# Staggering the K pairs of a down projection and releasing their loads product by product

## The chip, the cores and the metric

One core of a Trainium2 chip runs the whole program; seven cores are idle. The metric is the device time of one execution in microseconds. The engines are TensorE (PE in the profile, its weight loads PEld), VectorE (DVE), ScalarE (ACT), GpSimd (POOL, used here only to issue DMAs) and SyncE (SP, which issues DMAs too).

## The reference

A decoder trunk on x of 1024 tokens by 1024 channels, float32: one short-convolution layer and one attention layer (multi-head latent attention with 8 heads), each followed by a gated feed-forward block, and a final normalisation. What the change touches is the second half of the feed-forward block, which runs twice:

```python
def swiglu_ffn(h, w13, w2):
    g, u = jnp.split(h @ w13, 2, axis=-1)
    return (jax.nn.silu(g) * u) @ w2          # (1024 x 2816) @ (2816 x 1024)

h = h + swiglu_ffn(rms_norm(h, conv_ffn_norm_g[i]), conv_ffn_w13[i], conv_ffn_w2[i])
h = h + swiglu_ffn(rms_norm(h, mla_ffn_norm_g[j]), mla_ffn_w13[j], mla_ffn_w2[j])
```

## The kernel before

Activations are kept transposed: 128 channels on the partitions, 1024 tokens along the row, in tiles of 4 KB a partition. Every float32 operand is split into a high and a low float32r part, so one product of two blocks is three matmuls (high·high, high·low, low·high).

Feed-forward products go by a seven-product scheme (Strassen's, in Winograd's form) on 2 by 2 blocks: a **K pair** (256 of the inner dimension), two output blocks of 128 channels and two token halves of 512. `pair()` (line 145) does one **step**: for two output blocks it runs through the seven products in the order of `SEQ` (1, 5, 6, 2, 7, 3, 4), and in each through the K pairs that it is given. A step over three K pairs is 7 x 3 x 3 = 63 matmuls of 128x512, over two pairs 42. For each product `source()` mixes the four raw weight blocks on VectorE (tiles `w` and `sums`; line 155 adds two of them, 158, 161 and 165 subtract), `split()` casts the result on ScalarE (line 92) and takes the rest on VectorE (line 93) into `wo`, and after the matmuls `hook()` takes the bank away. Products 1, 6, 7 and 4 follow each other in the bank of tile `ps_z` and 5 and 3 in that of `ps_y`: the next product adds to the same bank, so TensorE can't start it before `hook()` has read the bank. Weight blocks are loaded by SP (line 140) into `wraw`, 10 tiles of 2 KB, of which a step with three pairs takes 5.

`ffn()` (line 682) first makes the inner activations: `up()` runs once for each of 22 blocks of 128 inner channels (a step over four K pairs, 84 matmuls), and after each second block `operands()` (line 256) puts eleven small VectorE instructions, with casts on ScalarE, on `queue`; `drip()` takes one from there after each product. They make the seven operands `x` of one K pair, which POOL stores to memory (`md`, 512 KB each). The last pair made (`KEPT`, pair 4) stays on chip.

`back()` (line 475) is the down projection, 11 K pairs by 8 output blocks, 16 steps. `GROUPS` cuts the pairs into (0,1), (2,3,4), (5,6,7), (8,9,10); each group runs through four steps (`mp`, two output blocks each) before the next group starts. In the first group ScalarE copies four of the seven products into `h` and VectorE adds three; later VectorE adds all seven (line 500). While a group runs, the operands of the next are asked for (`xm` from `md`, on POOL's queue, line 85): some after each step, the rest after the fourth. All these tiles share 41 slots (`NSLOT`): a load whose slot isn't free waits on POOL's queue for the matmul that reads it last. In the third group SP also loads `hs`, the residual.

The order on each engine is made at compile time by a scheduler that simulates the engines' times; a tile's next load waits for its last reader by a semaphore. POOL and SP issue in order; all transfers share 16 DMA engines.

Of the kernel before, what the change touches and what calls it, by code (L numbers as in the profile page):

```python
# [36 lines left out]
GROUPS = ((0, 1), (2, 3, 4), (5, 6, 7), (8, 9, 10))  # L37
KEPT = 4
PREFETCH = 4
# [15 lines left out]
def trunk(ctx, tc, aps, out):  # L55
# [28 lines left out]
    def move(dst, src):  # L84
        nc.gpsimd.dma_start(dst, src)  # L85
# [44 lines left out]
    def raw_blocks(w, kps, c1, c2):  # L130

        nk = len(kps)
        wv = w.rearrange("(k h p) n -> p h k n", p=P, h=2)
        R = {}
        for q, (kh, c, key) in enumerate(((0, c1, "11"), (0, c2, "12"), (1, c2, "22"), (1, c1, "21"))):
            if nk > 2 or q % 2 == 0:
                t = wraw("w" + key)
            else:
                t = t[:, HS // 2:]
            nc.sync.dma_start(t[:, :nk * P].rearrange("p (k m) -> p k m", m=P), wv[:, kh, kps[0]:kps[0] + nk, c:c + P])  # L140
            R[key] = t
        return R

    def pair(w, kps, X, c1, c2, hook, seq=SEQ):
# [27 lines left out]
        for name in seq:  # L172
            o = wop("wo" + name)
            hi, lo = part(o, n)
            split(hi, lo, source(name))
# [8 lines left out]
            hook(name, b)  # L184
            drip(1 if len(queue) < 14 else 2)

    def blocks(w, X, c1, c2, emit, seq=SEQ):
# [3 lines left out]
        def hook(name, b):  # L191
            if name in "156":
                kept[name] = half("z" + name)
                nc.scalar.copy(out=kept[name], in_=b)  # L194
            elif name == "2":
                emit("11", b, kept["1"])
            elif name == "3":
                emit("12", b, kept["6"])
            elif name == "7":
                emit("22", b, kept["5"])  # L200
            else:
                emit("21", b, None)
# [27 lines left out]
    def take(dst, ps, add):  # L230
        if add is None:
            nc.scalar.copy(out=dst, in_=ps)
        else:
            nc.vector.tensor_tensor(dst, ps, add, ALU.add)  # L234
# [240 lines left out]
    def back(w, load, st, final, ready, kept):  # L475
# [3 lines left out]
        for gi, g in enumerate(GROUPS):  # L479
            todo = []  # L480
            if gi + 1 < len(GROUPS):
                nxt = GROUPS[gi + 1]
                new = [{} for _ in nxt]
                if KEPT in nxt:
                    new[nxt.index(KEPT)] = kept
                todo = [(i, kp, name) for name in SEQ for i, kp in enumerate(nxt) if kp != KEPT]
            pace = -(-(NSLOT - KD - 2 - 7 * (len(g) + (gi == 0))) // 3)
            for mp in range(KD // 2):
                n1, n2 = 2 * mp, 2 * mp + 1
                if gi == 0:  # L490
                    st[n1], st[n2] = slot("h"), slot("h")
                h1, h2 = st[n1], st[n2]
                dst = {"1": h1[:, T1], "2": h1[:, T1], "6": h1[:, T2], "3": h1[:, T2],
                       "7": h2[:, T2], "5": h2[:, T2], "4": h2[:, T1]}

                def hook(name, b):
                    if gi == 0 and name in "1654":
                        nc.scalar.copy(out=dst[name], in_=b)
                    else:
                        nc.vector.tensor_tensor(dst[name], b, dst[name], ALU.add)  # L500
                    if gi == len(GROUPS) - 1 and name == "3":
                        final(mp, 2)

                pair(w2, g, ready, n1 * P, n2 * P, hook)
                n = len(todo) if mp == KD // 2 - 1 else min(len(todo), pace)
                for i, kp, name in todo[:n]:
                    new[i][name] = load(kp, name)
                todo = todo[n:]
                if gi == len(GROUPS) - 2:
                    for m in (n1, n2):  # L510
                        t = slot("hs")
                        nc.sync.dma_start(t, hd[m])
                        queue.append(lambda m=m, t=t: nc.vector.tensor_tensor(st[m], st[m], t, ALU.add))
                if gi == len(GROUPS) - 1:
                    final(mp, 1)
            if gi + 1 < len(GROUPS):
                ready = new
                drip()

# [162 lines left out]
    def ffn(w13, w2, X, after, side=None):  # L682
# [3 lines left out]
        def load(kp, name):  # L686
            o = slot("xm", F32R, [P, 2, HS])
            move(o, md[kp, SEQ.index(name)])
            return o

        def up(j):
# [3 lines left out]
            def emit(blk, ps, add):  # L695
                if blk in ("11", "12"):
                    take(a[:, T1 if blk == "11" else T2], ps, add)
                elif blk == "22":
                    take(u2, ps, add)
                else:  # L700
                    got["u1"] = ps
# [16 lines left out]
        ready, kept = [{} for _ in GROUPS[0]], {}  # L718
        order = [k for kp in range(KF // 2) if kp != KEPT for k in (2 * kp, 2 * kp + 1)] + [2 * KEPT, 2 * KEPT + 1]
        for j in order:  # L720
            up(j)
            if j % 2:
                put = kept.__setitem__ if j // 2 == KEPT else lambda name, o, j=j: move(md[j // 2, SEQ.index(name)], o)
# [11 lines left out]
        back(w2, load, st, after(st), ready, kept)  # L735
# [483 lines left out]
```

## Time and profile before

| | |
|---|---|
| median of 3 runs | 2104.06 us (2101.93 to 2107.01) |
| profiled execution | 2109.98 us, span of its instructions 2108.0 us |
| granted TensorE clock over the span | 0.992 |
| TensorE busy | 2071.3 us (98%) |
| VectorE, ScalarE busy | 1624.9 us (77%), 932.0 us (44%) |
| first down projection | about 779 to 989 us of the span |
| second down projection | about 1862 to 2088 us |

Times in the rows are microseconds from the start of the span, mean durations in ns. "Busy" counts an engine's instructions; a busy TensorE isn't TensorE at its peak. A granted clock of 1.00 is 2.4 GHz, half of it 1.2 GHz. A DMA share is the mean busy share of the core's 16 DMA engines, and may pass 1 where packets overlap.

### The profile page before, as it was taken

Reading aid. Unit: us, or ns where it says so; the run is one execution under the profiler, and the core shown is the slowest. Engines: PE = TensorE matmul, PEld = TensorE weight load, DVE = VectorE, ACT = ScalarE, POOL = GpSimd, SP = SyncE. Lnnn points to the kernel's source line nnn. Section 1 sums busy time; section 2 is a strip of 40 time slices with the busy share of each in tenths; the row PEclk is TensorE's granted clock in tenths of the full one; section 3 lists DMA queues with packets and bytes.
Section 4 is the critical chain, followed back from the end, with each engine's and each line's share of the span. In section 5 each row is a group of like instructions: output and inputs, shape, how many; then the busy total and the mean of one; then the engine's idle time right before and its main releaser. Section 6 shows DMA issues by size and latency. Waiting matters only on the chain.

```text
span 2108.0 us, 27158 instructions
## 1 busy us (share of the span) xinstructions
PE 2071.3 (98%) x9606; PEld 1721.6 (82%) x9606; DVE 1624.9 (77%) x2662; ACT 932.0 (44%) x1697; POOL 230.5 (11%) x440
## 2 busy tenths in 40 slices
PE   8999999999999999999999999999999999999998
PEld 6878887888888887788888888887888888878786
DVE  5797757789988887689558877767888888876775
ACT  6633344444444443224445555455444444442235
POOL 1000100000101121110001011100010010121100
PEclk9999999999999999999999999999999999999998
DMA  6133462343544587764222124532454454686751
GB/s 248 35 97 119 141 214 91 120 147 123 185 140 156 174 302 262 258 226 133 85 69 66 38 66 122 178 101 62 140 170 148 133 173 144 216 280 203 268 185 80
DMA packets 263399, 321.24 MB, mean 152 GB/s; under 512 B 18959, under 2 KB 207568, under 8 KB 263264
## 3 DMA queue, kind: packets, MB, share of 16 engines
q0 software_dynamic: 57792, 201.46, 28.0%
q1 hardware_dynamic: 205472, 118.07, 19.0%
q8 instruction: 75, 1.23, 0.2%
q14 instruction: 60, 0.49, 0.1%
HBM read 206.22 MB, written 108.00 MB: 149 GB/s over the span
## 4 chain that ended last, share of the span: by engine, by line
PE 92%; DVE 3%; DMA 2%; ACT 1%; issue 1%; SPq 0%; POOL 0%; POOLq 0%; DVEq 0%; ACTq 0%
PE ps_z L180 37%; PE ps_y L180 27%; PE ps_c L225 7%; PE ps_s L948 4%; PE ps_pv L983 2%; PE ps_t L972 1%; PE ps_wo L105 1%; PE ps_wo L107 1%; PE ps_wo L109 1%; PE ps_l L109 1%; PE ps_l L105 1%; PE ps_l L107 1%; DMA w<-in_mla_ffn_w_dram 1%; PE ps_q L105 1%; PE ps_q L107 1%
## 5 line engine op out<-in xcount | busy, mean ns | idle before, releaser
L180 PE MATMUL ps_z<-x,wo 128*128 128x512 f32 x2532 | 609.9, 390 | 3.6 <-ACT z L194 2.8
L180 PEld LDWEIGHTS ps_z<-x,wo 128*128 128x128 f32 x2532 | 475.5, 188 | 104.7 <-ACT z L194 4.1
L180 PE MATMUL ps_y<-x,wo 128*128 128x512 f32 x1764 | 432.3, 389 | 1.2 <-DVE x L93 0.9
L180 PEld LDWEIGHTS ps_y<-x,wo 128*128 128x128 f32 x1764 | 330.6, 188 | 70.9 <-DVE x L93 1.8
L92 ACT CAST wo<-w 128x512 fp32r<-128x512 f32 (+2 forms) x423 | 238.6, 570 | 281.1 <-PE ps_y L180 110.5
L93 DVE TENSOR_TENSOR wo<-w,wo 128x512 fp32r<-128x512 f32 (+2 forms) x423 | 260.8, 623 | 62.2 <-ACT wo L92 61.4
L180 PE MATMUL ps_z<-xm,wo 128*128 128x512 f32 x960 | 241.9, 395 | 7.9 <-DVE h L500 5.9
L180 PEld LDWEIGHTS ps_z<-xm,wo 128*128 128x128 f32 x960 | 180.8, 190 | 50.5 <-DVE h L500 7.8
L92 ACT CAST wo<-sums 128x512 fp32r<-128x512 f32 (+2 forms) x172 | 98.3, 572 | 260.9 <-PE ps_y L180 101.7
L180 PE MATMUL ps_y<-xm,wo 128*128 128x512 f32 x720 | 182.6, 392 | 2.3 <-DVE h L500 2.3
L180 PEld LDWEIGHTS ps_y<-xm,wo 128*128 128x128 f32 x720 | 135.2, 189 | 31.8 <-DVE h L500 3.1
L85 POOL DMA_DIRECT2D md<-x x140 | 75.0, 536 | 738.1 <-DVE x L93 695.6
L194 ACT COPY z<-ps_z 128x512 f32<-128x512 f32 x106 | 62.0, 585 | 136.5 <-PE ps_z L180 136.4
L93 DVE TENSOR_TENSOR wo<-sums,wo 128x512 fp32r<-128x512 f32 (+2 forms) x172 | 107.4, 624 | 14.2 <-ACT wo L92 12.9
L500 DVE TENSOR_TENSOR h<-ps_z,h 128x512 f32<-128x512 f32 x104 | 71.5, 688 | 40.5 <-PE ps_z L180 39.6
L85 POOL DMA_DIRECT2D xm<-md x140 | 74.1, 536 | 260.1 <-PE ps_z L180 138.3
L93 DVE TENSOR_TENSOR x<-t,x 128x512 fp32r<-128x512 f32 x136 | 92.2, 686 | 5.7 <-ACT x L92 5.7
L234 DVE TENSOR_TENSOR a<-ps_y,z 128x512 f32<-128x512 f32 x88 | 60.7, 689 | 42.3 <-PE ps_y L180 42.1
L92 ACT CAST x<-t 128x512 fp32r<-128x512 f32 x136 | 82.4, 620 | 20.8 <-DVE t L249 20.2
L955 ACT ACTIVATE p<-ps_s,mx,qscale 128x128 f32<-128x128 f32 (+3 forms) x64 | 53.4, 835 | 70.7 <-DVE mx L954 66.7
L155 DVE TENSOR_TENSOR sums<-w,w 128x512 f32<-128x512 f32 (+2 forms) x85 | 53.3, 627 | 31.3 <-DMA w<-in_mla_ffn_w_dram 15.1
L500 DVE TENSOR_TENSOR h<-ps_y,h 128x512 f32<-128x512 f32 x88 | 60.4, 686 | 20.7 <-PE ps_y L180 20.5
(295 smaller groups left out, 3213.6 us busy)
## 6 DMA issues: line engine op xcount, KB each, us to landing
md<-x POOLq DMA_DIRECT2D x140, 512.0 KB, 3.5
xm<-md POOLq DMA_DIRECT2D x140, 512.0 KB, 8.1
w<-in_conv_ffn_w_dram SPq DMA_DIRECT2D x88, 256.0 KB, 2.9
w<-in_mla_ffn_w_dram SPq DMA_DIRECT2D x88, 256.0 KB, 3.0
w<-in_conv_w_in_dram SPq DMA_DIRECT2D x48, 256.0 KB, 3.1
hd<-h POOLq DMA_DIRECT2D x24, 512.0 KB, 3.5
w<-in_conv_ffn_w_dram SPq DMA_DIRECT2D x48, 192.0 KB, 4.7
w<-in_mla_ffn_w_dram SPq DMA_DIRECT2D x48, 192.0 KB, 4.4
```

Of the source, the lines that this page charges most:

```text
L85: nc.gpsimd.dma_start(dst, src)
L92: nc.scalar.copy(out=hi, in_=src)
L93: (eng or nc.vector).tensor_tensor(lo, src, hi.bitcast(F32), ALU.subtract)
L105: nc.tensor.matmul(ps[:, hs], lhsT=wh, rhs=xh(k)[:, hs], start=st, stop=False)
L107: nc.tensor.matmul(ps[:, hs], lhsT=wh, rhs=xl(k)[:, hs], start=False, stop=False)
L180: mm = lambda w_, x_, f: nc.tensor.matmul(b, lhsT=w_[:, m], rhs=x_, start=f, stop=True, skip_group_check=True)
L194: nc.scalar.copy(out=kept[name], in_=b)
L225: nc.tensor.matmul(ps[:, ts], lhsT=w_[:, m], rhs=X[i][f"b{kh}{th}"][:, q, :], start=st and j == 0, stop=en and j == 2)
L234: nc.vector.tensor_tensor(dst, ps, add, ALU.add)
L500: nc.vector.tensor_tensor(dst[name], b, dst[name], ALU.add)
L948: nc.tensor.matmul(ps[:, a:b], lhsT=q[:, qs], rhs=k[:, a:b], start=i == 0, stop=i == 4 and b < kw)
L955: nc.scalar.activation(p, ps[:, :kw], AF.Exp, bias=mx, scale=qscale[:, qb:qb + 1], accum_out=rsum)
```

## The change

`GROUPS` becomes `SETS`, eight sets of K pairs that run through two steps each. A pair still has four steps, one for each two output blocks, but pairs enter and leave in turn: pair 1 runs steps 2 to 5, pair 2 steps 4 to 7, and so on. Pair 10 runs in the first two steps and in the last two, so its seven operands are loaded twice. The kept pair is pair 3 in place of 4; the inner activations of pair 10 are made first, those of pair 3 last. Since `SEQ0` goes with block 0, the first `up()` now runs in the order of `SEQ`.

Loads: the operands of the first set are asked for one at a time by the products of the last two `up()` steps; the other 63 by `pace()`, load *i* after product 1.5 *i* of the down projection (*i* below 14) or 10 + 4/3 *i*. Each such load waits by a semaphore for the instruction that took that product's bank away. Before, nothing but slots held them.

In the first four steps each weight mix and split is put behind the bank reads of four products earlier on its engine (an edge for the scheduler, no semaphore), and `drip()` is called after three products of step 0 and four of each of steps 1 to 3, in place of all seven.

```diff
-GROUPS = ((0, 1), (2, 3, 4), (5, 6, 7), (8, 9, 10))
-KEPT = 4
-PREFETCH = 4
+SETS = ((0, 10), (0, 1), (1, 2, 3), (2, 3, 4), (4, 5, 6), (5, 6, 7), (7, 8, 9), (8, 9, 10))
+KEPT = 3
+AHEAD = 4
+PACE = (1.5, 10, 4 / 3)
...
+    marks, paced = [], deque()
+    @contextmanager
+    def behind(n):
+        with ExitStack() as stack:
+            seen = set()
+            for inst in reversed(marks[:max(0, len(marks) - n + 1)][-4:]):
+                if inst is not None and inst.ins.engine not in seen:
+                    seen.add(inst.ins.engine)
+                    stack.enter_context(tc.issue_after(inst.ins))
+            yield
...
-    def pair(w, kps, X, c1, c2, hook, seq=SEQ):
+    def pair(w, kps, X, c1, c2, hook, seq=SEQ, thin=SEQ, ahead=99):
...
-            split(hi, lo, source(name))
+            with behind(ahead):
+                split(hi, lo, source(name))
...
-            hook(name, b)
-            drip(1 if len(queue) < 14 else 2)
+            marks.append(hook(name, b))
+            if paced and marks[-1] is not None:
+                paced.popleft()(marks[-1])
+            if name in thin:
+                drip(1 if len(queue) < 14 else 2)
...
+        todo = []
+        for q in range(1, len(SETS)):
+            new = [k for k in SETS[q] if k != KEPT and k not in SETS[q - 1]]
+            todo += [(kp, name) for name in SEQ for kp in new]
+        nload, products = len(todo), [0]
+        def pace(i):
+            return PACE[0] * i if i < 14 else PACE[1] + PACE[2] * i
+        for t in range(2 * len(SETS)):
+            mp, kps = t % (KD // 2), SETS[t // 2]
+            first, last = t < KD // 2, t >= 2 * len(SETS) - KD // 2
...
+            def hook(name, b):
+                if first and name in "1654":
+                    done = nc.scalar.copy(out=dst[name], in_=b)
+                else:
+                    done = nc.vector.tensor_tensor(dst[name], b, dst[name], ALU.add)
...
+                while todo and pace(nload - len(todo)) <= products[0]:
+                    kp, nm = todo.pop(0)
+                    ready.setdefault(kp, {})[nm] = load(kp, nm, done)
+                products[0] += 1
+                return done
+            if t % 4 == 0 and t:
+                drip()
+            pair(w2, kps, [ready[kp] for kp in kps], n1 * P, n2 * P, hook, thin=("1", "5", "6") if t == 0 else SEQ[::2] if first else SEQ, ahead=AHEAD if first else 99)
...
-        def load(kp, name):
+        def load(kp, name, behind=None):
             o = slot("xm", F32R, [P, 2, HS])
-            move(o, md[kp, SEQ.index(name)])
+            d = move(o, md[kp, SEQ.index(name)])
+            if behind is not None:
+                tc.add_manual_dep(d.ins, behind.ins.name, SYNC)
             return o
...
-            if j == order[-3]:
+            if j in order[-3:-1]:
+                kp = SETS[0][j == order[-2]]
                 for name in SEQ:
-                    ready[0][name] = load(GROUPS[0][0], name)
-        for name in SEQ:
-            for i, kp in enumerate(GROUPS[0]):
-                if i:
-                    ready[i][name] = load(kp, name)
+                    paced.append(lambda done, kp=kp, name=name: ready[kp].__setitem__(name, load(kp, name, done)))
+        while paced:
+            paced.popleft()(None)
```

## Rows read from the trace of the kernel before

**Rows 1.** The page's first part: busy time of each engine, share, instructions.
```profile
PE 2071.3 (98%) x9606; PEld 1721.6 (82%) x9606; DVE 1624.9 (77%) x2662; ACT 932.0 (44%) x1697; POOL 230.5 (11%) x440
```

**Rows 2.** TensorE's waits, 770 to 1000 us: line, awaited; total us, times, longest.
```profile
PE ps_z L180 <- DVE h L500: 2.9, 1, 2.9
PE ps_z L180 <- ACT wo L92: 1.1, 1, 1.1
PE ps_z L180 <- DVE wo L93: 0.5, 1, 0.5
```

**Rows 3.** TensorE's waits, 1845 to 2070 us.
```profile
PE ps_z L180 <- DVE h L500: 3.0, 1, 3.0
PE ps_y L180 <- DVE h L500: 2.0, 1, 2.0
```

**Rows 4.** Busy time by stretch: us, then each engine (x), PEclk, DMA share, GB/s.
```profile
780.00:790.00 10.00, 9.76 (x42) 7.44 (x41) 9.29 (x18) 6.82 (x15) 3.69 (x7) 1.00 1.13 389
...
874.00:882.00 8.00, 8.00 (x29) 6.39 (x28) 5.28 (x11) 1.25 (x3) 1.58 (x3) 0.79 1.11 406
882.00:890.00 8.00, 8.00 (x37) 6.60 (x36) 4.83 (x9) 2.28 (x5) 1.06 (x2) 1.00 1.11 390
...
930.00:940.00 10.00, 10.00 (x46) 8.29 (x45) 7.65 (x15) 2.47 (x5) 1.45 (x3) 1.00 1.12 391
...
1870.00:1880.00 10.00, 9.24 (x32) 7.02 (x32) 8.73 (x19) 4.52 (x11) 1.05 (x2) 0.83 1.13 399
...
1959.00:1967.00 8.00, 8.00 (x30) 6.40 (x29) 5.31 (x11) 1.30 (x3) 1.60 (x4) 0.79 1.11 403
```

**Rows 5.** The chain that ended last, in order of time: start us, us, what.
```profile
863.88 8.48 DMA w<-in_conv_ffn_w_dram
...
889.45 4.08 PE ps_z L180 x18
...
1861.50 7.87 DMA w<-in_mla_ffn_w_dram
...
1948.74 8.58 DMA w<-in_mla_ffn_w_dram
```

**Rows 6.** VectorE in order of time, from 852 us; idle time and releaser bracketed.
```profile
872.48 0.56 DVE L155 TENSOR_TENSOR sums<-w,w 128x384 f32<-128x384 f32 x1 [4.39 <-DMA w<-in_conv_ffn_w_dram]
872.96 0.68 DVE L500 TENSOR_TENSOR h<-ps_z,h 128x512 f32<-128x512 f32 x1
```

**Rows 7.** POOL in order of time, 855 to 885 us.
```profile
859.11 1.19 POOL L85 DMA_DIRECT2D xm<-md  x2 [34.24 <-PE ps_z L180]
...
870.66 0.53 POOL L85 DMA_DIRECT2D xm<-md  x1 [0.15 <-issue]
```

**Rows 8.** DMA queues, 860 to 872 us: packets, MB, share of 16 engines.
```profile
q0 software_dynamic: 928, 3.41, 86.1%
q1 hardware_dynamic: 878, 0.43, 14.2%
```

**Rows 9.** Weight loads of line 140, 843 to 858 us.
```profile
DMA to landing us min/median/max: 2.6/2.6/2.6
```

**Rows 10.** All instructions on tile xm: loads from issue to landing.
```profile
DMA to landing us min/median/max: 3.4/8.1/13.2
```

**Rows 11.** Busy time by stretch: the two down projections.
```profile
779.00:989.00 210.00, 205.13 (x890) 167.48 (x889) 163.98 (x290) 73.55 (x144) 30.73 (x59) 0.99 0.70 234
1862.00:2088.00 226.00, 220.72 (x980) 179.88 (x978) 163.52 (x290) 84.68 (x165) 26.93 (x51) 0.98 0.59 196
```

**Rows 12.** VectorE by form, 779.5 to 798.5 us: count, busy us, mean ns, idle before.
```profile
L93 DVE TENSOR_TENSOR x<-t,x 128x512 fp32r<-128x512 f32 x4 | 2.7, 686 | 0.0
...
L93 DVE TENSOR_TENSOR x<-a,x 128x512 fp32r<-128x512 f32 x3 | 2.1, 686 | 0.0
```

**Rows 13.** TensorE at the first step of the first `up()`, in order of time.
```profile
359.82 3.01 PE L180 MATMUL ps_z<-x,wo 128*128 128x512 f32 x12 [1.19 <-ACT z L194]
```

More of the change, by code (lines that the diff above doesn't have):

```diff
@@ L1 @@
 from collections import deque
-from contextlib import ExitStack
+from contextlib import ExitStack, contextmanager
 import numpy as np
@@ L193, in hook @@
                 kept[name] = half("z" + name)
[L194 to L202, printed above, removed]
+                return nc.scalar.copy(out=kept[name], in_=b)
+            if name == "2":
+                return emit("11", b, kept["1"])
+            if name == "3":
+                return emit("12", b, kept["6"])
+            if name == "7":
+                return emit("22", b, kept["5"])
+            return emit("21", b, None)
         pair(w, range(len(X)), X, c1, c2, hook, seq)
@@ L472, in tables, with back @@
         move(trig[0], cos)
-    def back(w, load, st, final, ready, kept):
+    def back(w, load, st, final, ready):
         w2 = w.rearrange("a k n -> (a k) n")
[L479 to L517, printed above, removed]
-                drip()
@@ new lines, in back @@
+        todo = []
[7 more added lines that the diff above has]
+            mp, kps = t % (KD // 2), SETS[t // 2]
+            n1, n2 = 2 * mp, 2 * mp + 1
+            first, last = t < KD // 2, t >= 2 * len(SETS) - KD // 2
+            if first:
+                st[n1], st[n2] = slot("h"), slot("h")
+            h1, h2 = st[n1], st[n2]
+            dst = {"1": h1[:, T1], "2": h1[:, T1], "6": h1[:, T2], "3": h1[:, T2],
+                   "7": h2[:, T2], "5": h2[:, T2], "4": h2[:, T1]}
+            def hook(name, b):
[3 more added lines that the diff above has]
+                    done = nc.vector.tensor_tensor(dst[name], b, dst[name], ALU.add)
+                if last and name == "3":
+                    final(mp, 2)
+                while todo and pace(nload - len(todo)) <= products[0]:
[4 more added lines that the diff above has]
+            if t % 4 == 0 and t:
+                drip()
+            pair(w2, kps, [ready[kp] for kp in kps], n1 * P, n2 * P, hook, thin=("1", "5", "6") if t == 0 else SEQ[::2] if first else SEQ, ahead=AHEAD if first else 99)
+            if 8 <= t < 12:
+                for m in (n1, n2):
+                    x = slot("hs")
+                    nc.sync.dma_start(x, hd[m])
+                    queue.append(lambda m=m, x=x: nc.vector.tensor_tensor(st[m], st[m], x, ALU.add))
+            if last:
+                final(mp, 1)
@@ L696, in emit @@
                 if blk in ("11", "12"):
[L697 to L701, printed above, removed]
+                    return take(a[:, T1 if blk == "11" else T2], ps, add)
+                if blk == "22":
+                    return take(u2, ps, add)
+                got["u1"] = ps
             blocks(w, X, j * P, (KF + j) * P, emit, SEQ if j else SEQ0)
@@ L716, in up @@
             mid[j] = a
-        ready, kept = [{} for _ in GROUPS[0]], {}
-        order = [k for kp in range(KF // 2) if kp != KEPT for k in (2 * kp, 2 * kp + 1)] + [2 * KEPT, 2 * KEPT + 1]
+        ready = {kp: {} for kp in SETS[0] + (KEPT,)}
+        kpo = [SETS[0][1]] + [kp for kp in range(KF // 2) if kp not in (KEPT, SETS[0][1])] + [KEPT]
+        order = [k for kp in kpo for k in (2 * kp, 2 * kp + 1)]
         for j in order:
@@ L722, in ffn @@
             if j % 2:
-                put = kept.__setitem__ if j // 2 == KEPT else lambda name, o, j=j: move(md[j // 2, SEQ.index(name)], o)
+                put = ready[KEPT].__setitem__ if j // 2 == KEPT else lambda name, o, j=j: move(md[j // 2, SEQ.index(name)], o)
                 operands(mid.pop(j - 1), mid.pop(j), put)
```

12 lines of the change are left out of this document (6 added, 6 removed).

## The prediction

> **What bounds the kernel now.** I read the page's busy times first: TensorE is busy for 2071.3 of 2108.0 us [rows 1], so only its pauses, and stretches at a lower clock, can be won. Next its waits in the two down projections: 2.9 us at one place, 1.1 and 0.5 us at others in the first, 3.0 and 2.0 us in the second [rows 2, 3]; smaller ones are 0.2 us each. Then the clock by stretch: 0.79 over 8 us right after the first long pause, 0.83 over 10 us and 0.79 over 8 us after the two of the second projection, 1.00 in the others shown [rows 4]. A lost share of the clock is lost time: 0.21 x 8 = 1.7 us, 0.17 x 10 = 1.7 us, 1.7 us. The reader checks this by counts: 29 matmuls began in the 8 us after the pause, 37 in the next 8 [rows 4], and 8 x 4.08/18 = 8 x 0.227 us [rows 5] is 1.8 us. So the change has in reach
>
> - in the last step of the second group, once in each projection: 2.9 + 1.7 and 3.0 + 1.7 = **9.3 us**;
> - in the first steps: 1.1 + 0.5 in the first projection, 2.0 + 1.7 in the second = **5.3 us**.
>
> Why the long pauses? In the chain of waits they are weight loads: 8.48 and 8.58 us in flight, 7.87 us for that of the first steps [rows 5]; in a quiet stretch the same load lands after 2.6 us [rows 9]. VectorE sat 4.39 us on the first of them with a weight mix, and the bank read that TensorE waited for (`h<-ps_z`) stood right behind it in VectorE's order [rows 6]. The load was late because POOL had begun a run of twelve operand loads, from 859.11 to 870.66 us (the first and the last are shown), as pairs 2 and 3 left their slots together [rows 7]. In these 12 us POOL's queue moved 3.41 MB in 928 packets, SP's only 0.43 MB in 878 [rows 8].
>
> **The change part by part.**
>
> *The same work.* Old and new have four steps of two pairs and twelve of three: 4 x 42 + 12 x 63 = 924 matmuls, the same splits, the same bank reads. TensorE's floor stays.
>
> *Loads by pace.* A product is 9 matmuls, 2.04 us, with three pairs, and 6, 1.36 us, with two. One load per 4/3 products is one in 2.72 us, or in the first steps one per 1.5 products, in 2.04 us. When saturated the DMA engines move about 406 GB/s [rows 4], so a load of 512 KB (0.524 MB) holds them for 1.29 us: 47% and 63% of the time, where the old burst held them altogether. Weights ask for 0.786 MB per step of 14.3 us, 55 GB/s; hence there is room, also where `hs` adds two loads of 512 KB to a step (73 GB/s; 193 + 55 + 73 = 321 of 406). How late may a weight load be? The one of 8.48 us cost TensorE 2.9, so 5.6 us would have cost nothing. Under a burst it takes 8.5, alone 2.6; at about half the load I take the middle, 5.5, or less. That is under the limit, though barely; but the limit is the tightest one: from 930 to 940 us the engines were saturated (1.12) and TensorE was busy for all 10.00 us [rows 4]. I take the two long pauses away whole: **-9.3 us** (bounds: 0, if the bursts stay, and -9.3).
>
> *The last `up()` steps and the first steps.* Here fourteen loads, until now in two runs of seven and one of twelve behind, are spread over two `up()` steps (38 us); 780 to 790 us was at a DMA share of 1.13 [rows 4], which falls, since the twelve are spread as well. The kept pair's operands are made now while three or four, not seven, queue entries fall to a step: in 19 us VectorE did seven operand splits of 0.69 us [rows 12] besides their mixes and was busy for 9.29 of 10 us [rows 4]. With the thinner queue one operand falls into step 0, four into step 1, two into step 2; they are needed in step 4, so nothing waits for them. Step 1 stays nearly full on VectorE, so I don't take all: half of 1.6 us in the first projection, and 2.0 + 1.7 less a rest of 1.0 in the second: **-3.5 us** (bounds: 0 and -5.3).
>
> *Edges.* `behind(4)` adds no instruction. It can hold a split back by some products; with five `wo` tiles a split can't run further ahead than five anyway. 0, and if it leaves a split late, the nearest price is a wait for a split, 0.5 to 1.1 us [rows 2], for each projection: up to +2.2.
>
> *The added wait.* Each load now waits on POOL for a bank read. Behind it on POOL stand the next loads, the stores of pair 9's operands and in the end `hd`. Nobody but later loads waits for the stores. The loads' own margin is least at the last load for step 8: it is number 34, due after product 55.3, issued at the 57th, and needed by the 63rd, five whole products or 10.2 us later; likewise in step 12. Loads landed after 8.1 us in the median, 13.2 at the longest, which was in a saturated queue [rows 10]. Free if the queue is paced: 0 (bound: 13.2 - 10.2 = 3.0 us at two places of two projections, +12).
>
> *Seven more loads a projection* (pair 10 twice): 14 x 1.29 = 18 us of DMA time, while the engines are at 0.70 and 0.59 in the projections [rows 11]. They lie under matmuls: 0; bare they would cost 18.
>
> *The first `up()`* runs 2 before 3. The pause that the old order shows, 1.19 us, comes at its third product [rows 13], which both orders share: 0, with ± one product of 12 matmuls (2.7 us) in each block as bounds.
>
> *Slots.* Steps 12 and 13 need 21 operands, 7 arriving, 8 `h`, four `xh`/`xl` and two for the statistics, 42 of 41; pair 7 leaves at that very time, and the last load has 11 products. 0.
>
> **Sum:** -9.3 - 3.5 = -12.8. On the profiled execution's own time, 2109.98 - 12.8 = 2097.2 us. That execution is 5.9 us above the median of the runs, 2104.06. If the surplus lies elsewhere, the median becomes 2104.06 - 12.8 = 2091.3; if it lies in these very pauses, 2104.06 - 6.9 = 2097.2. I can't tell which, and stand between, a little nearer to the first: **2093.5 us**.
>
> **The rivals.**
>
> *A. The pace doesn't bind.* A load still needs a slot, and if slots free up later than the pace asks, POOL's order and its bursts stay. For: the old burst was released by slots, its waits are for TensorE's products [rows 7]. Against: now one or two pairs leave per two steps, not three in one step. Then only the first steps gain: 2104.06 - 3.5 = 2100.6 us.
>
> *B. Operands late.* The margin of 10.2 us is less than the longest landing [rows 10]. At two places per projection, 3.0 us each, the gain goes: 2104.06 - 12.8 + 12 = 2103.3. Against: landings of that length came in runs of a dozen.
>
> *C, on the other side: weights late everywhere.* The old bursts left long quiet stretches, in which weights landed in 2.6 us [rows 9]; the paced queue leaves none, so that each three-pair step meets operand loads. If a mix that stands ahead of bank reads waits for longer than 5.6 us, it costs what the old ones cost, 2.9 + 1.7 = 4.6 us. It decides from the third such pause on (12.8 / 4.6 = 2.8) among 24 three-pair steps; with four it is 2104.06 - 12.8 + 18.4 = 2109.7 us. For: my middle of 5.5 lies 0.1 us from the limit, and SP's queue got 36 GB/s (0.43 MB in 12 us) beside POOL's [rows 8]. Against: 930 to 940 us.
>
> The Trainium skill speaks for C: its page "DMA: Bandwidth & Descriptors", in "Queues, rings and completion order", says that each DMA engine takes turns between the queues that have work, a packet at a time. The trace agrees, with 878 packets beside 928 [rows 8]; by that rule alone a small-packet queue loses whenever any load is in flight, paced or not, and the result would be C's 2109.7 us. The same page's "Rules for kernel authors" advises to issue a DMA early and wait late, which the pace goes against; by it B's 2103.3 us would come out.
>
> **How the numbers follow.** The forecast 0.64; A 0.11; B 0.10; C 0.10; 0.05 for a gain of more than all 14.6 us in reach. About 0.2% (4.2 us) can be told from no change here: faster is below 2099.9, slower above 2108.3. The forecast and the larger gain are faster, with a fifth of A and B, 0.73; C is slower in nine of ten cases, 0.09, and B's tail adds 0.01, 0.10; the rest, 0.17, is the same. The forecast's own range is 2088 to 2099. The range: below, 2104.06 - 14.6 - 2 (the spread of three runs to the lower side is 2.1) = 2087; above, it takes in A and B, 2104.
>
> **What would show it.** In the changed profile: no pause above 1 us of TensorE between the fourth and the ninth step of a down projection, weight loads below 5.6 us there, a granted clock of 1.00 through both projections, POOL's `xm` issues 2 to 3 us apart in place of runs, and waits on POOL released by ScalarE and VectorE bank reads and not by TensorE. In the first steps under 1 us of pause each. Wrong would be: `h` or `wo` waits of 2 us and more at other steps (C), TensorE waiting for a DMA on `xm` (B), runs of loads 0.7 us apart (A).

## The result, and the profile after

The changed kernel is slower: 2114.5 us, median of fifteen runs (2110.12 to 2122.4), against 2105.04 (2099.16 to 2109.38) for the kernel before beside it. The ratio is 1.005, with 95% from 1.004 to 1.0059. Forecast was 2093.5, with a range that ended at 2104.

The two profiled executions hide this. That of the changed kernel took 2110.12 us, the fastest of its fifteen; that of before, 2109.98, is above all fifteen of its later runs. Their spans agree within 0.3 us. What follows is read first from this pair, stretch by stretch, and then from a second profile of each.

The busy times of the changed kernel (engine, us, share, instructions), beside [rows 1]: the same 9606 matmuls, 14 more instructions on POOL.

```profile
PE 2068.3 (98%) x9606; PEld 1719.7 (82%) x9606; DVE 1626.2 (77%) x2662; ACT 929.7 (44%) x1697; POOL 237.7 (11%) x454
```

TensorE's waits in the changed kernel, 770 to 1000 and then 1845 to 2095 us (line, awaited; total, times, longest):

```profile
PE ps_z L197 <- DVE h L521: 6.2, 3, 3.2
PE ps_z L197 <- ACT h L519: 0.4, 1, 0.4
...
PE ps_z L197 <- DVE h L521: 6.1, 3, 2.3
...
PE ps_z L197 <- ACT h L519: 0.4, 1, 0.4
```

The waits of [rows 2] and [rows 3] are gone: no `wo`, no 2.0 us in the first steps, no long pause near 873 or 1958. But there are six new ones, all on a bank read of VectorE, all late in the projection: at 913.75, 945.77 and 963.64 us, and at 1998.94, 2029.87 and 2046.35. They come to 13.1 us with the short ones, against 4.9 + 5.2 = 10.1 in that profile of before (its waits of 0.2 us taken in). The clock fell once in the two projections, not three times as in [rows 4], so that the sums nearly cancel:

```profile
945.00:953.00 8.00, 7.23 (x25) 5.78 (x26) 7.11 (x14) 1.03 (x2) 1.05 (x2) 0.79 0.61 175
```

(Columns as in [rows 4]: 1.7 us of clock lost behind the pause of 3.16 us.) The place is steps 10, 12 and 13. What ran there is shown by the chain of waits of the changed kernel, in order of time (start us, us, what):

```profile
936.11 7.68 DMA hs<-hd
...
945.77 3.83 PE ps_z L197 x9
...
955.04 5.54 DMA w<-in_conv_ffn_w_dram
...
963.64 2.33 PE ps_z L197 x9
```

Two kinds of late transfer stop VectorE: the residual (`hs`, 7.68 us in flight) and a weight block (5.54 us). VectorE itself, in order of time with its idle time and releaser in brackets:

```profile
943.88 1.23 DVE L537 TENSOR_TENSOR h<-h,hs 128x1024 f32<-128x1024 f32 x1 [4.62 <-DMA hs<-hd]
945.03 0.68 DVE L521 TENSOR_TENSOR h<-ps_z,h 128x512 f32<-128x512 f32 x1
...
960.70 0.56 DVE L171 TENSOR_TENSOR sums<-w,w 128x384 f32<-128x384 f32 x1 [2.06 <-DMA w<-in_conv_ffn_w_dram]
...
1997.13 0.56 DVE L171 TENSOR_TENSOR sums<-w,w 128x384 f32<-128x384 f32 x1 [3.33 <-DMA w<-in_mla_ffn_w_dram]
...
2027.98 1.23 DVE L537 TENSOR_TENSOR h<-h,hs 128x1024 f32<-128x1024 f32 x1 [3.49 <-DMA hs<-hd]
```

The residual's add (line 537) sat 4.62 us at the head of VectorE's order, and the bank read that TensorE needed (line 521) stood right behind it, as a weight mix had done in [rows 6]. Of the six pauses two (3.16 and 2.03 us) stand behind such an add and three (1.67, 1.80 and 2.31 us) behind a weight mix that waits for its load; for the one at 913.75 us (1.40) the profile names no releaser. VectorE's waits of 4.62, 3.49 and 3.33 us cost TensorE 3.16, 2.03 and 1.80: all but 1.5 us. So it was before, when 4.39 [rows 6] cost 2.9 [rows 2].

The residual was not late because it flew for longer. Its loads and adds in the first projection (count: ns min/median/max, first and last start in us), before, then changed:

```profile
L512 SPq DMA_DIRECT2D hs<-hd x8: 338/339/362, 876.2 to 931.6; - x8
L513 DVE TENSOR_TENSOR h<-h,hs x8: 1218/1220/1227, 897.4 to 944.3; 128x1024 f32<-128x1024 f32 x8
...
DMA to landing us min/median/max: 3.7/9.0/12.2
```

```profile
L536 SPq DMA_DIRECT2D hs<-hd x8: 338/350/570, 891.6 to 936.6; - x8
L537 DVE TENSOR_TENSOR h<-h,hs x8: 1219/1223/1228, 898.4 to 946.4; 128x1024 f32<-128x1024 f32 x8
...
DMA to landing us min/median/max: 5.2/6.8/9.7
```

In the old kernel the loads took longer to land, but four of the eight were issued 21 to 30 us ahead of their adds and four 5 to 13; in the changed one all were issued 5 to 10 us ahead, VectorE's waits taken in. VectorE reached the add of the longest pause at 939.26 us, 3.2 us after its load was issued (936.11); in the old kernel it came to the same add 10 us after the issue. VectorE's waits for DMAs in that projection (total us, times, longest), before, then changed:

```profile
DVE sums L155 <- DMA w<-in_conv_ffn_w_dram: 9.6, 6, 4.4
...
DVE h L513 <- DMA hs<-hd: 0.5, 1, 0.5
```

```profile
DVE h L537 <- DMA hs<-hd: 6.6, 3, 4.6
DVE sums L171 <- DMA w<-in_conv_ffn_w_dram: 5.1, 6, 2.1
```

Over both projections VectorE waited 20.8 us for weight blocks before and 13.5 after, so the change did help them; for the residual it waited 2.4 us before and 11.5 after. The DMA queues from 895 to 935 us (packets, MB, share of 16 engines), first the changed kernel, then that before:

```profile
q0 software_dynamic: 2011, 7.33, 55.9%
q1 hardware_dynamic: 4718, 5.03, 39.9%
```

```profile
q0 software_dynamic: 1345, 4.92, 36.1%
q1 hardware_dynamic: 4451, 3.10, 27.4%
```

Together 12.4 MB against 8.0 MB. By stretches (columns as in [rows 4]), the changed kernel and that before:

```profile
895.00:935.00 40.00, 38.60 (x171) 31.64 (x170) 32.67 (x55) 9.47 (x19) 7.11 (x14) 1.00 0.96 310
935.00:965.00 30.00, 25.17 (x103) 20.00 (x102) 20.31 (x33) 9.25 (x15) 5.81 (x11) 0.94 0.86 274
```

```profile
895.00:935.00 40.00, 40.00 (x178) 33.15 (x177) 32.63 (x55) 9.73 (x19) 6.86 (x13) 1.00 0.64 202
935.00:965.00 30.00, 30.00 (x134) 24.60 (x133) 27.76 (x47) 10.87 (x18) 1.07 (x2) 1.00 0.57 190
```

The old kernel left the DMA engines a third of their time idle in these 40 us, since from 880 to 975 us its operand loads waited 28.6 us on POOL's queue for the residual's adds, which free slots; the changed one, whose operand loads wait 1.1 us for the residual, put them there, and the share is 0.96. The weight loads of 895 to 965 us, the changed kernel and that before (rows of line 143 and of line 140):

```profile
DMA to landing us min/median/max: 2.5/5.5/11.3
```

```profile
DMA to landing us min/median/max: 2.6/3.9/8.6
```

POOL's issues do follow the pace: mostly one or two at a time, 2.5 to 4 us apart, released by bank reads and not by TensorE as in [rows 7]. POOL of the changed kernel, in order of time:

```profile
870.08 0.53 POOL L86 DMA_DIRECT2D xm<-md  x1 [2.95 <-DVE h L521]
872.58 0.53 POOL L86 DMA_DIRECT2D xm<-md  x1 [1.96 <-DVE h L521]
876.66 1.05 POOL L86 DMA_DIRECT2D xm<-md  x2 [3.55 <-DVE h L521]
```

The second profiles, of runs of 2123.02 us (changed) and 2103.53 us (before), show the difference that the first pair hid, and more than that: the first profile of the changed kernel is of the fastest of its fifteen runs, the second is above them all. TensorE's waits in the two projections, changed, then before:

```profile
PE ps_z L197 <- DVE h L521: 10.2, 5, 5.2
...
PE ps_z L197 <- DVE h L521: 7.5, 4, 3.6
```

```profile
PE ps_z L180 <- DVE h L500: 0.5, 1, 0.5
...
PE ps_y L180 <- DVE h L500: 2.0, 1, 2.0
PE ps_z L180 <- DVE h L500: 1.6, 1, 1.6
```

The changed kernel waits 17.7 us on bank reads, with 5.2 us at one place, behind an add of the residual (5.40 us of wait). Its DMA share of 895 to 935 us is lower than in the first profile:

```profile
895.00:935.00 40.00, 37.67 (x165) 30.56 (x164) 28.53 (x49) 9.04 (x18) 7.24 (x14) 1.00 0.89 280
```

The old one waits 0.5 and 1.6 us where [rows 2] and [rows 3] had 2.9 and 3.0, and only one of its three drops of the clock is left. So the two long pauses, on which three quarters of the forecast gain rested, took 9.3 us with the clock behind them in one profile and 2.1 us in the other.

### The profile page after: what moved, and what is told of

The parts are those of the page before. It is cut to its first block, busy times and chain, and to the rows that moved or that the text cites. A ratio compares the mean times of both kernels' runs of the same rounds, so it can differ in the third digit from the quotient of the medians.

```text
span 2108.3 us, 27148 instructions
## 1 busy us (share of the span) xinstructions
PE 2068.3 (98%) x9606; PEld 1719.7 (82%) x9606; DVE 1626.2 (77%) x2662; ACT 929.7 (44%) x1697; POOL 237.7 (11%) x454
## 4 chain that ended last, share of the span: by engine, by line
PE 87%; DVE 5%; DMA 3%; issue 3%; ACT 1%; POOL 0%; SPq 0%; POOLq 0%; ACTq 0%; DVEq 0%
PE ps_z L197 34%; PE ps_y L197 25%; PE ps_c L244 7%; PE ps_s L971 4%; PE ps_pv L1006 2%; PE ps_t L995 1%; PE ps_wo L108 1%; PE ps_wo L110 1%; PE ps_wo L112 1%; DMA w<-in_conv_ffn_w_dram 1%; PE ps_l L112 1%; PE ps_l L108 1%; PE ps_l L110 1%; PE ps_q L108 1%; PE ps_q L110 1%
## 5 line engine op out<-in xcount | busy, mean ns | idle before, releaser
L197 PE MATMUL ps_z<-xm,wo 128*128 128x512 f32 x960 | 242.1, 394 | 13.8 <-DVE h L521 12.4
L197 PEld LDWEIGHTS ps_z<-xm,wo 128*128 128x128 f32 x960 | 179.4, 189 | 57.0 <-DVE h L521 12.6
L86 POOL DMA_DIRECT2D xm<-md x154 | 81.5, 531 | 357.0 <-DVE h L521 249.3
L96 DVE TENSOR_TENSOR wo<-sums,wo 128x512 fp32r<-128x512 f32 (+2 forms) x172 | 107.7, 626 | 14.5 <-ACT wo L95 13.1
L731 ACT ACTIVATE a<-a 128x1024 f32<-128x1024 f32 x44 | 46.7, 1061 | 63.1 <-DVE a L730 62.8
L734 DVE TENSOR_TENSOR a<-a,R 128x1024 f32<-128x1024 f32 x44 | 53.9, 1225 | 25.8 <-ACT a L731 25.8
```

Source lines behind the costliest of these rows:

```text
L86: return nc.gpsimd.dma_start(dst, src)
L96: (eng or nc.vector).tensor_tensor(lo, src, hi.bitcast(F32), ALU.subtract)
L197: mm = lambda w_, x_, f: nc.tensor.matmul(b, lhsT=w_[:, m], rhs=x_, start=f, stop=True, skip_group_check=True)
L734: nc.vector.tensor_tensor(a, a, get_R(), ALU.mult)
```

## The experiments

Theories at the start. **T1**: the changed kernel is slower because `hd`'s residual loads now share steps 8 to 11 with paced operand loads, so that weights and residual land late. **T2**: the residual's adds, at a bad place in VectorE's order, are the cause and not their traffic. **T3**: the pace itself is to blame, or the staggering, or the first steps' edits. Each ratio is to the kernel before, beside which the run stood. The scheduler orders the engines anew for every edit, so that an edit can move the time by its order too.

**The residual left out.** Two kernels without its loads and adds (this part of the result is not computed).

```
-            if 8 <= t < 12:                      (changed; before: if gi == len(GROUPS) - 2)
-                for m in (n1, n2):
-                    x = slot("hs")
-                    nc.sync.dma_start(x, hd[m])
-                    queue.append(... tensor_tensor(st[m], st[m], x, ALU.add))
```

> The changed kernel, with the residual left out of both down projections: no hs loads (8 of 512 KB in each) and no adds of them. Theory 1 (crowded DMA: in steps 8 to 13 the paced operand loads, the weights and hs together ask for all the DMA engines can move, VectorE then waits in order for hs or weights, and TensorE behind it): the pauses of steps 8 to 13 mostly go, about 2114 - 10 = 2104 us, and less than 4 us from the old kernel without its residual. Theory 2 (the cost is in the order of the first steps, edges and thinner queue): still 8 to 10 us above the old kernel without its residual, about 2112. Theory 3 (the waits added to POOL's queue themselves cost time): about 2112 as well.

> The old kernel, with the residual left out of both down projections in the same way; it is what the run before this one is compared with. Theories 1, 2 and 3 all expect 0 to 4 us less than the old kernel, 2101 to 2105 us, since its two long pauses stood in the last step of the second group, before any hs load.

Measured: 2096.55 us, 0.9953 (0.9941 to 0.9966), and 2108.74 us, 1.0023 (1.0012 to 1.0034). Without the residual the change gains 12.2 us between the medians; with it, it loses 9.5. The whole loss needs the residual. That 12.2 is close to the forecast of 12.8 bears out no single term: the first steps' edits alone gain 6 (below), and against the old kernel with its residual the gain is 9.0. That the old kernel became 3.2 us slower without its residual was not expected and is not explained; a worse order is a possibility that no run here tests.

**Its loads without its adds, and its adds without its loads** (in the first the residual is not added; in the second `st` is added to itself).

```
-                    queue.append(lambda m=m, x=x: nc.vector.tensor_tensor(st[m], st[m], x, ALU.add))
```

```
-                    x = slot("hs")
-                    nc.sync.dma_start(x, hd[m])
-                    queue.append(lambda m=m, x=x: nc.vector.tensor_tensor(st[m], st[m], x, ALU.add))
+                    queue.append(lambda m=m: nc.vector.tensor_tensor(st[m], st[m], st[m], ALU.add))
```

> The changed kernel with the hs loads kept and their adds left out (the tiles are loaded and not read): DMA traffic as in the change, VectorE has 8 adds of 1.2 us fewer in each projection, and nothing waits for hs. If the traffic is what costs (theory 1a), weight mixes still wait and about half of the loss or more stays, 2106 to 2114 us. If the adds are (a VectorE with 9.8 us more work in steps 8 to 12, and its waits for hs; theory 1c), the result is that without any residual, 2096 to 2100 us.

> The changed kernel without hs loads, but with adds of the same size in their places (h is added to itself): VectorE's work as in the change, the traffic 4.2 MB smaller in each projection. Theory 1a: as without any residual, 2096 to 2101 us. Theory 1c: 2106 to 2114 us. If it takes both, each of these two runs is near 2100 us.

Measured: loads alone 2106.92 us (eleven runs, 2098.89 to 2115.11), 1.0009 (0.9995 to 1.0022); adds alone 2097.25 us, 0.9961 (0.9948 to 0.9974). The adds' work costs 0.7 us over the kernel without either (2096.55), the loads' traffic 10.4, and a further 7.6 come with both, when adds can wait for loads. With the loads alone VectorE waits 15.9 us for weight blocks in the two projections, with the adds alone 4.2. TensorE's waits with the adds alone (770 to 1000, 1845 to 2095 us):

```profile
PE ps_z L197 <- DVE h L521: 1.4, 1, 1.4
...
PE ps_z L197 <- DVE h L521: 1.3, 1, 1.3
```

and with the loads alone:

```profile
PE ps_z L197 <- DVE h L521: 3.3, 1, 3.3
...
PE ps_z L197 <- DVE h L521: 2.5, 1, 2.5
```

The DMA share of 895 to 935 us is 0.80 with the adds alone and 0.97 with the loads alone:

```profile
895.00:935.00 40.00, 40.00 (x178) 33.12 (x177) 34.12 (x58) 9.94 (x20) 8.46 (x16) 1.00 0.80 245
```

```profile
895.00:935.00 40.00, 40.00 (x178) 33.15 (x177) 28.85 (x52) 10.24 (x20) 7.93 (x15) 1.00 0.97 327
```

T1 holds for 10.4 of the 18.0 us. The other 7.6 need loads and adds together; that they are the adds' waits in VectorE's order (T2) agrees with the trace, but no run took these waits away alone.

**Moving the residual.** Three attempts to keep the change and place the residual better: its adds put on the queue a step later; its loads on POOL's queue; its loads spread over eight steps.

```
+            queue.extend(held)
+            held = []
...
-                    queue.append(lambda m=m, x=x: ...)
+                    held.append(lambda m=m, x=x: ...)
```

```
-                    nc.sync.dma_start(x, hd[m])
+                    move(x, hd[m])
```

```
-            if 8 <= t < 12:
-                for m in (n1, n2):
+            if 4 <= t < 12:
+                for m in ((n1,) if t < 8 else (n2,)):
```

> The changed kernel; each hs tile is still loaded after its step of the third quarter, but its add is put on the queue one step later. The DMA traffic stays. Theory 1 with the add as the blocker: the waits of VectorE for hs go (6.6 and 4.9 us in the profile) and with them the pauses that stand behind them, 2108 to 2111 us. Theory 1 with the weights as the only blocker, and theories 2 and 3: no change, 2112 to 2117 us.

> The changed kernel with the eight hs loads of each projection issued by POOL in place of SP: the same volume, but no hs ahead of a weight block in SP's queue; it stands among the operand loads instead. Theory 1b: weight blocks land in under 5.6 us and the pauses behind them go, 2104 to 2109 us. Theory 1a: the same volume gives the same time, 2111 to 2118 us.

> The changed kernel with one hs tile per step over steps 4 to 11 in place of two per step over steps 8 to 11: the same volume, half the rate. Theory 1a: by shares of DMA time (operand loads 58%, weights 22%, hs 22%, in sum 102% before) it is 91% now, and most pauses go, 2098 to 2106 us. If even that is too full, 2110 us or more.

Measured: 2118.01 us, 1.0054 (1.0042 to 1.0066); 2112.27 us, 1.0043 (1.003 to 1.0056); 2111.21 us, 1.0044 (1.0032 to 1.0057). None helps beyond its interval. The first and the third miss what I expected. The first did not move the adds: the scheduler put them back. In both traces VectorE's instructions from 870 to 960 us stand in the same order, the adds begin at 897.4 to 944.9 us against 898.4 to 946.4, and VectorE waits 12.9 us for the residual against 11.5. So this is in effect the changed kernel again, 3.5 us above its median, and the adds' place stays untested. With the loads on POOL's queue VectorE's waits for the residual fall to 3.6 us and those for weight blocks rise to 21.8; TensorE still pauses for up to 2.9 us. Halving the residual's rate over twice the steps leaves pauses of 2.6 and 3.4 us, with waits of 8.1 and 21.1 us.

**Less other traffic.** Pair 10 is loaded once only (the last two steps use pair 9's operands twice: pair 10's part of those is left out), seven loads fewer a projection.

```
-            todo += [(kp, name) for name in SEQ for kp in new]
+            todo += [(kp, name) for name in SEQ for kp in new if not (kp == 10 and q == len(SETS) - 1)]
```

> The changed kernel without the second load of pair 10: in the last two steps the operands of pair 9 stand in for it (seven loads of 512 KB fewer in each projection, the same matmuls). Theory 1a (volume: in steps 8 to 13 loads, weights and hs ask for more than the DMA engines can move): the queue is emptier by some 1.6 us of its time per load from step 12 on, so the pauses of steps 12 and 13 shrink, 2105 to 2110 us. Theory 1b (place: hs stands in SP's queue ahead of the weight blocks): little changes, 2111 to 2115 us.

Measured: 2111.53 us, 1.0033 (1.0021 to 1.0046), at most 3 us better than the changed kernel, and the intervals overlap. The seven loads are not the main cost.

**The pace.** The waits taken off (loads issued as slots allow), and a pace that runs ahead of the residual's steps.

```
-                    ready.setdefault(kp, {})[nm] = load(kp, nm, done)
+                    ready.setdefault(kp, {})[nm] = load(kp, nm)
```

```
-            return PACE[0] * i if i < 14 else PACE[1] + PACE[2] * i
+            return 1.5 * i if i < 14 else 4 + 4 / 3 * i if i < 45 else 64 + 1.75 * (i - 45)
```

> The changed kernel without the wait of the down projection's loads for a product's bank read: they are traced at the same places and keep the staggered sets, but only slots hold them back. Theory 1a: loads then run ahead of their products as far as slots allow, and leave the engines emptier in steps 8 to 13; fewer pauses there, some back in the first steps, 2104 to 2112 us. Theory 3 (the added wait itself costs): 2100 to 2105 us. If the pace is what keeps pauses away: 2118 us or more.

> The changed kernel with another pace: load i after product 1.5 i below 14, then 4 + 4/3 i up to load 44, then 64 + 1.75 (i - 45): six products earlier up to step 8, and 44% of the DMA engines' time in place of 58% beside hs. Theory 1a: 44 + 22 + 22 = 88%, the late pauses shrink, 2098 to 2106 us. If a moved pace only moves the pauses, 2110 us or more.

Measured: 2107.42 us, 1.0017 (1.0008 to 1.0026), and 2119.81 us, 1.0063 (1.0047 to 1.0079). The pace itself costs 7 us. Without it the late pauses are gone but for one of 0.5 us, and one early one is left in each projection, 4.5 and 3.7 us, each with a drop of the clock:

```profile
826.39 4.18 PE ps_z L197 x9
```

In that chain the pause ends a weight load issued at 811.39 us that took 11.48 us, in a stretch (812 to 824 us) at a share of 1.13. A burst, then, hurts once and a pace three times. But the edit changed a second thing. The residual's loads and adds in this kernel, first projection:

```profile
L536 SPq DMA_DIRECT2D hs<-hd x8: 338/339/364, 875.3 to 927.7; - x8
L537 DVE TENSOR_TENSOR h<-h,hs x8: 1216/1217/1219, 899.1 to 944.5; 128x1024 f32<-128x1024 f32 x8
```

Each load is issued 14 to 25 us ahead of its add, not 5 to 10 as in the changed kernel, and VectorE never waits for the residual. The DMA share of 895 to 935 us is 0.87. Which of the two gives the 7 us back, emptier engines or the earlier residual, is open: no run moved the residual's issue alone, and why the order of the paced kernel puts it so late is not shown. The pace moved ahead missed: it made nine pauses, up to 4.5 us.

**The first steps.** Undone in the changed kernel, and put alone into the kernel before.

```
-            pair(..., hook, thin=("1", "5", "6") if t == 0 else SEQ[::2] if first else SEQ, ahead=AHEAD if first else 99)
+            pair(..., hook, thin=SEQ, ahead=99)
```

```
-                pair(w2, g, ready, n1 * P, n2 * P, hook)
+                pair(w2, g, ready, n1 * P, n2 * P, hook, thin=("1", "5", "6") if gi == 0 and mp == 0 else SEQ[::2] if gi == 0 else SEQ, ahead=AHEAD if gi == 0 else 99)
```

> The changed kernel without its edits to the first steps: no edges behind bank reads (the edge is 99 products back, as in all other steps) and one queue entry after each product. Theory 2: the loss goes, about 2105 us. Theories 1 and 3: the pauses of the first steps come back, 2 to 5 us more than the changed kernel, 2116 to 2120 us.

> The old kernel (old groups, loads held by slots alone) with the edits of the first steps alone: edges behind the bank reads of four products earlier, thinner queue. In the changed kernel they were worth 11 us. The pauses of the first steps (1.6 us, and 2.0 + 1.7 in the second projection) go, the two long ones of 4.6 stay: 2100 us; if the burst is merely met elsewhere, 2104 us.

Measured: 2125.86 us, 1.0091 (1.0079 to 1.0103), and **2098.92 us, 0.9968 (0.9956 to 0.998)**. These edits are worth 11.4 us inside the changed kernel (more than the 2 to 5 expected) and 6 alone. The second kernel, old groups and old loads with thinner first steps and splits in order, beats both. Its waits of TensorE in the two projections, at a granted clock of 1.00 from 779 to 1000 and from 1862 to 2060 us:

```profile
PE ps_z L196 <- DVE h L517: 1.5, 1, 1.5
PE ps_z L196 <- ACT h L515: 0.3, 1, 0.3
...
PE ps_z L196 <- DVE h L517: 1.1, 1, 1.1
...
PE ps_z L196 <- ACT h L515: 0.3, 1, 0.3
```

**Pace and staggering apart.** The changed kernel with the old groups, paced; and staggered, paced for the first 21 loads alone.

```
-SETS = ((0, 10), (0, 1), (1, 2, 3), (2, 3, 4), (4, 5, 6), (5, 6, 7), (7, 8, 9), (8, 9, 10))
-KEPT = 3
+SETS = ((0, 1), (0, 1), (2, 3, 4), (2, 3, 4), (5, 6, 7), (5, 6, 7), (8, 9, 10), (8, 9, 10))
+KEPT = 4
```

```
-            return PACE[0] * i if i < 14 else PACE[1] + PACE[2] * i
+            return 1.5 * i if i < 21 else 0
```

> The changed code with the old grouping: sets (0,1), (2,3,4), (5,6,7), (8,9,10) of four steps each, pair 4 kept, nothing loaded twice (70 loads), with the pace and the edits of the first steps. It closes the square of grouping by pace (both with the first-step edits): old groups without pace 2098.9, staggered without pace 2107.4, staggered with pace 2114.5 us. If the pace costs whatever the grouping, by holding loads back into the steps with hs: 2103 to 2108 us. If only staggered sets with their pace crowd those steps: 2097 to 2101 us.

> The changed kernel with the pace kept for the first 21 of its 63 loads (load i after product 1.5 i) and dropped for the rest, which only slots hold back then. Theory: the pace helps in the first six steps, where loads without it delay a weight block by 11 us, and harms in steps 8 to 13. Expected: the late pauses stay away as without any pace, and the early one of 4.5 + 1.7 us in each projection goes too, 2107.4 - 12 = 2095 to 2100 us. If the loads then form a burst elsewhere: 2104 us or more.

Measured: 2111.47 us, 1.0036 (1.0022 to 1.0049), and 2109.05 us, 1.002 (1.0011 to 1.003). Both missed. The first is above both ranges that I gave; its residual too is issued 6.9 us ahead of its first add, and VectorE waits 14.4 us for it. The last one was expected to be faster than before: several pauses of 0.4 to 1.9 us replace the long ones, the sum of all waits on bank reads still 8 us. Four kernels, all with the first steps' edits, now stand in a square: old groups without the pace 2098.92 and with it 2111.47, staggered without 2107.42 and with 2114.5. The pace costs 12.6 or 7.1 us, the staggering 8.5 or 3.0 (by the ratios to the kernel beside them 14 or 7, and 10 or 3; the intervals of the last pair overlap). (The unpaced kernel with the old groups also keeps the old order of the first loads, so its side of the square differs in that too.)

**Second profiles of the two kernels**, read in the section above.

> The changed kernel once more, for a second profile: its first was that of its fastest run, 2110.12 us of 2110.12 to 2122.4. In a run near 2114.5 us the waits of TensorE in the two projections should be 3 to 6 us longer in sum than the 14.8 of the first profile, or the clock lower at one to three more places, all in steps 8 to 13.

> The old kernel once more, for a second profile: its first was that of a slow run, 2109.98 us, above all 15 runs timed later. In a run near 2104 us the pauses should sum to 4 to 6 us less than in the first profile.

Measured: 2123.02 and 2103.53 us, one run each.

## Why the prediction was wrong

**The failed step: "hence there is room, also where `hs` adds two loads of 512 KB to a step (73 GB/s; 193 + 55 + 73 = 321 of 406)".** The bytes came out, 310 GB/s in the first profile after; the room for small loads did not. The sum adds bytes per time, as if each byte cost the engines the same. The rows it had beside it say otherwise: in [rows 8] POOL's queue moves 284 GB/s for 86.1% of the engines, 330 GB/s at a full share, and SP's weights 36 GB/s for 14.2%, 252 GB/s at a full share. By these prices 193 of operands is 58%, 55 of weights 22%, and 73 of residual, priced as operands, 22%: 102%. Saturated stretches reach a share of 1.11 to 1.13 [rows 4], so that is nine tenths of what the engines can do, and not 79%. The traces after show 0.96 and 0.89 over the 40 us of these steps. With the residual's loads alone VectorE waited 15.9 us for weight blocks, with no residual 4.4, and the kernel was 10.4 us slower.

**The limit of 5.6 us failed with it.** It was taken from a load's time in flight. My 5.5 "in the middle" was met as a median, 11.3 was the longest; but the load that landed after 5.54 us, inside the limit, still cost TensorE 1.67 us (at 963.64, with an operand split of 1.2 us between the mix and the bank read). What counts is how long VectorE stands waiting: at most 1.5 us of it was free, as [rows 2] and [rows 6] already showed with 2.9 for 4.39.

**What came in its place** is in part rival C's mechanism, in steps 10 to 13 and not everywhere: three of six pauses stand behind weight mixes. In sum, though, VectorE waited less for weights than before (13.5 us against 20.8), not more. C had 2109.7 us; the median is 4.8 above. The Trainium skill's "DMA: Bandwidth & Descriptors", section "Queues, rings and completion order", which stood beside C, says that queues with work share the engines by turns. The runs agree in the direction: without the residual, at a share of 0.82, weight loads landed after 4.8 us in the median, against 2.6 in a quiet stretch [rows 9]. But there they cost TensorE no pause over 0.7 us, so that rule alone does not give the loss.

**A blocker that I did not list:** the residual's add. I treated `hs` as traffic alone; its adds stand in VectorE's order ahead of bank reads. With the pace its loads are issued 5 to 10 us ahead of them, where the old kernel issued half of them 21 to 30 us ahead, and two of the six pauses, the longest among them, stand behind such an add. Of the 18.0 us between the changed kernel and the one without the residual, 7.6 come only when loads and adds are both there.

**-9.3 us for the two long pauses: mis-sized.** The second profile of before has 0.5 and 1.6 us there, with no drop of the clock behind either. I noted that the profiled execution was 5.9 us above the median, and chose to believe that the surplus lay largely elsewhere. In the second profile 7.2 of the 9.3 us are absent, so it may well have lain in these pauses, for which I had 2097.2 us: still a gain. And the kernel with old bursts and the first steps' edits keeps pauses of 1.5 and 1.1 us there, without a pace.

**-3.5 us for the first steps: right in direction, too small.** They gain 6 alone, 11.4 within the change; my bound was 5.3. The pauses behind the first steps in the kernel that undoes them (2.20 and 1.47 us, and 1.05, 3.00 and 1.47) are longer than those of before, perhaps since paced loads keep VectorE's operands late there as well; that reason was only argued. The DMA share of 780 to 790 us did not fall, as I had said it would: it is 1.13 again.

**The added wait at 0, and B.** No wait of TensorE was put down to a DMA on `xm` in the changed kernel, so B's mechanism, operands late, is out. But the pace is not free: 7.1 and 12.6 us, while weights and residual are late. The Trainium skill's "DMA: Bandwidth & Descriptors", under "Rules for kernel authors", advises to issue early and wait late; the runs agree, with these 7.1 and 12.6 us, though not by the way in which I had B follow from it.

**Staggering, costed at 0** through "the same work": 3.0 us with the pace and 8.5 without. In the latter the trace names it, the early weight load of 11.48 us. With the pace, 3.0 us is not clear of the noise: the two intervals overlap.

**A** is out: POOL's issues follow the pace.

**The account**, from the medians: -6.1 (first steps, 2105.04 to 2098.92), +8.5 (staggering, to 2107.42), +7.1 (pace, to 2114.5): +9.5. Against the forecast's -12.8, the first term was 2.6 better, the other two 25 worse. These are differences between whole kernels, each with an order of its own; two kernels with the same order on VectorE stood 3.5 us apart, so steps of that size are not certain.

## What to carry to other kernels

Add up transfers in time of the DMA engines, each queue at its own price from a stretch of the trace, and ask of a smoothed schedule whether it fills a stretch that the burst had left free for something else. For each load that an engine waits for in order, compare its time to land with how far ahead of its use it is issued, after the change as well as before: here the residual landed sooner than before and was yet late. When an edit moves an instruction, look in the trace whether it moved. Before a gain is built on one pause, compare its execution with the median: where it is above all others, that pause may be why.

## What the runs showed of the hardware

- Beside a burst weight blocks cost the DMA engines about a third more time per byte than operand loads: 252 against 330 GB/s at a full share [rows 8]. Alone, from 843 to 858 us of the same profile (0.79 MB, 18.0%), they moved at about 290.
- The share of the DMA engines did not by itself tell whether TensorE would pause. At 0.80 to 0.82 (895 to 935 us, the adds alone and no residual) weight loads landed after 4.6 and 4.8 us in the median and TensorE lost at most 1.4 us at one place; at 0.96 and 0.97, with medians of 5.5 and 5.9, it lost 3 us and more. But the second profile of the changed kernel, at 0.89 with a median of 4.7, has a pause of 5.2 us, and the kernel without the pace, at 0.87 with 4.0, has no late one over 0.5.
- In these kernels a wait of VectorE ahead of a bank read cost TensorE all but 1.0 to 1.5 us of it, for the residual (4.62 us cost 3.16, 3.49 cost 2.03) as for weights (3.33 cost 1.80, 3.30 cost 2.31, and 4.39 cost 2.9 before); with an operand split in between, 2.06 cost 1.67.
- Two profiles of one kernel differ by more than the effect sought: the old kernel's pauses in the last step of the second group took 2.9 and 3.0 us in one, 0.5 and 1.6 in the other.
